# Sums of the second MLP weights: GpSimd instead of VectorE

## The chip, the cores and the metric

The kernel runs on one core of one Trainium2 chip. The metric is the device time of one execution in microseconds, the median of several runs. The core has TensorE (PE in the rows, with its weight loads as PEld), VectorE (DVE), ScalarE (ACT), GpSimd (POOL), and SyncE (SP), which in this kernel issues every DMA from one queue in the order of the program.

## What is computed

One residual block on 1024 tokens with 1024 channels: an adaLN-modulated norm, a combined input projection, two mixers (a gated linear recurrence and a short convolution), an output projection, and then the part that matters here, an MLP with 4096 hidden channels:

```
mod = silu(c) @ ada_w + ada_b                     # shift1, scale1, gate1, shift2, scale2, gate2
h   = rmsnorm(x, norm1_g) * (1 + scale1) + shift1
x   = x + gate1 * (mixers(h @ w_in) @ w_out)
h2  = rmsnorm(x, norm2_g) * (1 + scale2) + shift2
x   = x + gate2 * (square(relu(h2 @ w_mlp1)) @ w_mlp2)
out = rmsnorm(x, final_g)
```

## The kernel before

Every operand of a product is split in two float32r parts, a high one and a low one. `split` (L92 and L93) does it: ScalarE copies the source to the high part, and then VectorE writes source minus high part as the low part. Three matmuls (low weight, high weight, high weight with the low part of x; L97, L99, L101) make one product step.

Both MLP products are done by Strassen's scheme in Winograd's form. The work is cut into 16 pairs of quadruples of output tiles, `u` = 0 to 7 for the first MLP product and `u` = 8 to 15 for the second. Each pair needs seven products, P1 to P7, in the order 1, 6, 7, 4, 5, 3, 2. One product is 24 matmuls of 512 columns. The weights of a pair come as four blocks A11, A12, A21, A22, each [128, 1024] float32, and four sums of them are needed: S1 = A21 + A22, S3 = A11 - A21 and S2 = S1 - A11 in `sums`, and S4 = A12 - S2 in `sum4`. P6 takes S2, P7 takes S3, P5 takes S1 and P3 takes S4. The blocks and S1 share five buffers (G and four in F); S3 is written over A21, S2 over A11, S4 over S2. S2 can therefore only be made when A11 has been split for P1, and S4 when S2 has been split for P6.

`produce` makes the next weight operand, one for each product, into a ring of five slots. It is written when the product that used the slot five operands before has ended, so it is needed four products later.

In the second MLP product the x operands are sums of hidden tiles, which lie in DRAM (`hidd`). They are in four groups of two pairs. `load_hid` loads the next group's operands while the second pair of a group runs (u = 9, 11, 13; the first group's while u = 7 runs): for each of the seven products two halves, 14 in all, and each half is a DMA of 512 KB into one of two raw buffers, and a `split` from there. The two raw buffers are used in turn: `F[:, 24:26]` and `E[:, 2:4]`. A buffer is loaded again when VectorE has written the low part from it. These stretches are called windows below: window 1 is around u = 9, window 2 around u = 11, window 3 around u = 13; each reaches into the first products of the next pair. In a row, R<-E is the split of such a half from the E buffer. R<-F is either a half from the F buffer or a weight operand, R<-G is always a weight operand.

The result of a product stays in two PSUM banks. `acc2` (L963) on VectorE adds each bank into the residual: with P1, P6, P7 and P4 accumulating in the same two banks (as P5 and P3 do in two others), the next product may only write to a bank when `acc2` has read it. The first bank of a product is complete after half of its matmuls.

The order on each engine is not the order of the source: a list scheduler sets it with its own model of durations. Each engine then works strictly in that order.

Of the kernel before, what the change touches and what calls it, by code (L numbers as in the profile page):

```python
# [12 lines left out]
ALU = mybir.AluOpType  # L13

P = 128
# [8 lines left out]
# n-tiles of the input projection: 0-3 lx, 4-7 ly, 8-11 b, 12-15 c, 16-19 v.  # L24
# The first group is computed k-tile by k-tile while the modulation arrives.
# [3 lines left out]
# columns of the small vectors  # L29
# [6 lines left out]
def block_kernel(ctx, tc, xT, vec, adaT, winA, winB, gw, wout, w1, w2, outT):  # L36
# [8 lines left out]
    # R: operands of the products, each a pair of float32r parts; F: float32  # L45
# [7 lines left out]
    # two buffers that hold other things later  # L53
# [32 lines left out]
    def kc(k):  # L86
        """Columns of k-tile k in its half slot."""
        return slice(k % 4 * P, k % 4 * P + P)

    def split(dst, src):  # L90
        """dst: view [.., parts, ..] given as (hi, lo); the sum of the parts is src."""
        a = A(dst[0], src, AF.Copy)  # L92
        return a, V.tensor_tensor(dst[1], src, fp(dst[0]), op=ALU.subtract)  # L93

    def mm3(outs, wh, wl, start, stop, **kw):
        """outs: [(bank, x part hi, x part lo)]"""
        i = [T.matmul(b, lhsT=wl, rhs=xh, start=start, stop=False, **kw) for b, xh, xl in outs]  # L97
        for b, xh, xl in outs:
            T.matmul(b, lhsT=wh, rhs=xh, start=False, stop=False, **kw)  # L99
        for b, xh, xl in outs:  # L100
            T.matmul(b, lhsT=wh, rhs=xl, start=False, stop=stop, **kw)  # L101
        return i[0]
# [8 lines left out]
    def rsq(bank, r0, r1, n, act=nc.scalar.activation):  # L111
        # r0 = -2 n / sqrt(bank / n + EPS), one Newton step after the table
        act(r0, bank, AF.Abs_reciprocal_sqrt, bias=epsc, scale=1.0 / n)
        a = A(r1, r0, AF.Square)
        V.scalar_tensor_tensor(r1, bank, n * EPS, r1, op0=ALU.add, op1=ALU.mult)
        return a, V.scalar_tensor_tensor(r0, r1, -3.0 * n, r0, op0=ALU.add, op1=ALU.mult)
# [3 lines left out]
    def after(inst, prev):  # L120
        """inst is issued behind prev on their engine."""
        tc.add_manual_dep(ins_of(inst), ins_of(prev).name, NOSYNC, reason="order")
        return inst

# [43 lines left out]
    # softplus(a_param) = max(a, 0) + log1p(exp(-|a|))  # L168
# [19 lines left out]
    # the array clocks up while x comes in  # L188
# [9 lines left out]
    # order of adaT: (scale1, shift1) by k, gate1, (scale2, shift2) by k, gate2  # L198
# [58 lines left out]
    with tc.manual_schedule(engines={ET.DVE, ET.Activation, ET.SP}):  # L257
# [3 lines left out]
        # twice silu(c): c + c tanh(c / 2), then along the free dimension for all partitions  # L261
        cp = vt[:, V_C : V_C + KT]
        A(sc, cp, AF.Tanh, scale=0.5)
        # the table of the reciprocal root comes in before it is needed
# [13 lines left out]
        # norm1 of chunk 0: sums of squares, two tiles at a time  # L278
# [109 lines left out]
    # functions from the tables of ScalarE in one order, that keeps tables long  # L388
# [7 lines left out]
    def norm_out(n, cc, y, sqt, r1, bank, k):  # L396
        """y / rms of its group * gain, split into the slot of K-tile k."""
        A(sqt, y, AF.Square)
        dst = rs_(16 + 2 * k + cc)
        split(dst, sqt)  # L400
        T.matmul(bank, lhsT=bones, rhs=dst[0], start=True, stop=False)
        T.matmul(bank, lhsT=bones, rhs=dst[1], start=False, stop=True)  # L402
        rsq(bank, sqt, r1, 64, TA)
        V.scalar_tensor_tensor(y, y, gneg[:, n : n + 1], sqt, op0=ALU.mult, op1=ALU.mult)
        split(dst, y)
# [79 lines left out]
    # first group, chunk 0: out of PSUM, then chunk 1 with the same weights  # L485
# [103 lines left out]
    # the second gate waits for the hidden layer  # L589
# [3 lines left out]
    # ---- MLP: Strassen's products in Winograd's form, on 2 x 2 blocks of  # L593
    # (output channels) x (input channels) and (input channels) x (tokens).
    # Two quadruples of output tiles go side by side.
    # Weights: A11, A12, A21, A22; operands of the seven products:
    #   P1 A11 B11   P2 A12 B21   P3 S4 B22   P4 A22 T4   P5 S1 T1   P6 S2 T2   P7 S3 T3
    #   S1 = A21 + A22, S2 = S1 - A11, S3 = A11 - A21, S4 = A12 - S2
    #   T1 = B12 - B11, T2 = B22 - T1, T3 = B22 - B12, T4 = B21 - T2
    # first half slot and step of the operands, slots of the weights  # L600
# [4 lines left out]
    # the last pair ends on P4, P2, P5, P3, by halves of the tokens  # L605
# [12 lines left out]
    def pump():  # L618
        # keep one buffer for the sum S1 of the quadruples at hand
        while li[0] < len(loads) and comp_free:  # L620
            u, a = loads[li[0]]
            if len(comp_free) == 1 and any((v, 1) not in comp and (v, "S1 done") not in comp for v in range(u + 1) if (v, 22) in comp):
                break
            buf = comp_free.pop(0)
            kind, j = pairs[u]
            dma(buf, (w1 if kind == "w1" else w2)[j, {11: 0, 12: 1, 21: 2, 22: 3}[a]].rearrange("p (q b) -> p q b", q=2))
            comp[u, a] = buf
            li[0] += 1

    def sums(u):  # L630
        """All sums of the weights of pair u but S4."""
        if (u, 1) in comp or (u, "S1 done") in comp:
            return
        s1 = comp_free.pop(0)
        comp[u, 1] = s1
        comp[u, "S1 done"] = True
        V.tensor_tensor(s1, comp[u, 21], comp[u, 22], op=ALU.add)
        V.tensor_tensor(comp[u, 21], comp[u, 11], comp[u, 21], op=ALU.subtract)
        V.tensor_tensor(comp[u, 11], s1, comp[u, 11], op=ALU.subtract)

    def sum4(u):
        """S4, in the place of S2 or of A12, whichever is split already."""
        if (u, "S4") not in comp:
            t = comp[u, 11] if 6 in made[u] else comp[u, 12]
            V.tensor_tensor(t, comp[u, 12], comp[u, 11], op=ALU.subtract)
            comp[u, "S4"] = t
# [5 lines left out]
    def produce():  # L652
        """The next weight operand, split into the ring."""
        if wi[0] >= len(wseq):
            return
        u, p = wseq[wi[0]]
        slot = WR[wi[0] % 5]
        wslot[u, p] = slot
        wi[0] += 1
        pump()  # L660
        if p in (5, 6, 7, 3):
            sums(u)
        done = made.setdefault(u, set())
        dst = (R[:, slot : slot + 2, HI, :], R[:, slot : slot + 2, LO, :])
        if p == 3:
            sum4(u)
            split(dst, comp[u, "S4"])
        else:
            split(dst, comp[u, {1: 11, 2: 12, 4: 22, 5: 1, 6: 11, 7: 21}[p]])
        done.add(p)  # L670
        for a, users in ((11, {1, 6, 3}), (12, {2, 3}), (21, {7}), (22, {4}), (1, {5})):
            if (u, a) in comp and p in users and users <= done:
                comp_free.append(comp.pop((u, a)))
        pump()
# [4 lines left out]
    def xops(p, kp, cs=slice(0, H)):  # L679
        """Operands kp and kp + 1."""  # L680
        s0, st = XS[p]
        i = slice(s0 + kp * st, s0 + kp * st + st + 1, st)
        return R[:, i, HI, cs], R[:, i, LO, cs]

    # chunk 1 of the output projection, all but the first tile by halves of the
    # tokens; norm2 of what is done beside it
# [20 lines left out]
    def h2(cc, k, cs):  # L707
        """Tiles k and k + 1."""
# [6 lines left out]
    def t12(cs, steps):  # L715
        """h2 of chunk 1, T1, T2 and B22; steps go between."""
# [62 lines left out]
    def out_last():  # L779
        """The other half of the tokens, and the operands of the first half."""  # L780
# [165 lines left out]
    for u in range(8):  # L946
        if u == 7:
            # three pairs of tiles stay out of the last round, for x and the operands
# [23 lines left out]
    def block2(p, n0):  # L972
        """Chunk and tile that take the product p, or the sum that it ends."""
# [23 lines left out]
    # the last four products and the last norm, by halves of the tokens  # L997
# [80 lines left out]
def pack(i):  # L1078
    """Layout only: transposes, gathers of rows and columns, zero padding."""
# [28 lines left out]
    # blocks (output half, input half) of two quadruples: [pair][block][P][q][kp][P]  # L1108
    w1 = i["w_mlp1"][0].reshape(2, 4, P, 8, 2, 2, P)  # kh kp p pair q nh n
    w1 = f(w1.transpose(3, 5, 0, 2, 4, 1, 6).reshape(8, 4, P, D))  # L1110
    w2 = i["w_mlp2"][0].reshape(4, 4, 2, P, 2, 2, 2, P)  # g kp kh p half q nh n
# [22 lines left out]
```

## Time and profile before

| | us |
|---|---|
| median of 3 runs | 999.07 |
| the runs | 1000.42, 999.07, 993.2 |
| span of the profiled execution | 995.8 |
| TensorE busy in it | 968.8 |
| VectorE busy | 753.9 |
| ScalarE busy | 539.6 |
| GpSimd busy | 0.2 |

The profile's own time is given as its span alone, 995.8 us, which lies between the fastest run and the median. The page shows a busy time for each engine; it says little of a stage, since the two MLP products, the mixers and the start have different limits. The second MLP product runs from about 664 us to the end.

### The profile page before, as it was taken

How to read it: one execution, taken by the hardware profiler on the slowest of the kernel's cores; microseconds unless marked ns; L12 is line 12 of the kernel's file. 1: busy time of each engine (PE TensorE's matmuls, PEld its weight loads, DVE VectorE, ACT ScalarE, POOL GpSimd, SP SyncE). 2: the span in 40 equal slices, each digit the busy share in tenths (PEclk: the TensorE clock that was granted, in tenths of full speed). 3: DMA queues.
4: the chain of work that ended last, by engine and by line, in shares of the span. 5: the costliest groups of instructions: out<-in, count | busy, mean ns of one | idle time of the engine just before them, and what ended most of it. 6: DMA issues, size and time to landing. Idle time of an engine off the chain costs nothing.

```text
span 995.8 us, 11633 instructions
## 1 busy us (share of the span) xinstructions
PE 968.8 (97%) x4430; PEld 798.7 (80%) x4430; DVE 753.9 (76%) x1001; ACT 539.6 (54%) x719; POOL 0.2 (0%) x4
## 2 busy tenths in 40 slices
PE   8999999999999999999999999999999999999996
PEld 6878777778888988888888888887877878877886
DVE  7989788989545799776565564787797698598657
ACT  6769896874412677555455464682342253243444
POOL 0000000000000000000000000000000000000000
PEclk9999999999999999999999999999999999999999
DMA  8924015267322131773452444779554255155005
GB/s 308 345 93 146 1 44 190 67 214 262 113 106 96 49 118 58 254 271 142 155 195 101 169 169 140 282 249 321 169 180 140 97 188 180 66 188 169 1 1 168
DMA packets 53543, 154.50 MB, mean 155 GB/s; under 512 B 5104, under 2 KB 10736, under 8 KB 53488
## 3 DMA queue, kind: packets, MB, share of 16 engines
q1 hardware_dynamic: 53488, 153.77, 44.4%
q8 instruction: 34, 0.56, 0.2%
q14 instruction: 21, 0.17, 0.1%
HBM read 116.00 MB, written 37.75 MB: 154 GB/s over the span
## 4 chain that ended last, share of the span: by engine, by line
PE 69%; DMA 12%; DVE 10%; ACT 6%; issue 1%; SPq 0%; DVEq 0%; ACTq 0%
PE bank L97 23%; PE bank L99 22%; PE bank L101 22%; DMA E<-hidd 8%; DVE R L93 5%; ACT R L92 3%; DMA F<-hidd 2%; DMA F<-adaT 2%; ACT F L392 1%; DVE F L202 1%; DVE F L450 1%; DMA F<-xT 1%; DVE F L963 1%; ACT L392 1%; PE bank L402 1%
## 5 line engine op out<-in xcount | busy, mean ns | idle before, releaser
L97 PE MATMUL bank<-R 128*128 128x512 f32 (+1 forms) x1416 | 524.4, 382 | 10.7 <-DVE F L963 6.2
L99 PE MATMUL bank<-R 128*128 128x512 f32 (+1 forms) x1416 | 521.3, 379 | 0.0
L101 PE MATMUL bank<-R 128*128 128x512 f32 (+1 forms) x1416 | 516.6, 379 | 0.5 <-DVE R L93 0.5
L97 PEld LDWEIGHTS bank<-R 128*128 128x128 f32 x1416 | 266.7, 188 | 67.5 <-DVE F L963 10.8
L101 PEld LDWEIGHTS bank<-R 128*128 128x128 f32 x1416 | 266.8, 188 | 51.1 <-DVE R L93 1.0
L99 PEld LDWEIGHTS bank<-R 128*128 128x128 f32 x1416 | 266.8, 188 | 49.5 <-issue 0.7
L92 ACT ACTIVATE R<-F 128x1024 fp32r<-128x1024 f32 (+1 forms) x188 | 179.6, 965 | 178.7 <-PE bank L101 95.5
L93 DVE TENSOR_TENSOR R<-F,R 128x1024 fp32r<-128x1024 f32 (+1 forms) x188 | 205.5, 1109 | 72.4 <-ACT R L92 72.1
L963 DVE SCALAR_TENSOR_TENSOR F<-bank,md,F 128x512 f32<-128x512 f32 (+1 forms) x120 | 84.8, 712 | 36.3 <-PE bank L101 35.7
L92 ACT ACTIVATE R<-E 128x1024 fp32r<-128x1024 f32 x28 | 29.7, 1061 | 43.9 <-DMA E<-hidd 42.7
L878 ACT ACTIVATE F<-bank 128x512 f32<-128x512 f32 x44 | 26.2, 595 | 50.4 <-PE bank L101 49.1
L93 DVE TENSOR_TENSOR R<-E,R 128x1024 fp32r<-128x1024 f32 x28 | 34.3, 1224 | 12.2 <-ACT R L92 11.6
L93 DVE TENSOR_TENSOR R<-G,R 128x1024 fp32r<-128x1024 f32 x23 | 28.1, 1222 | 12.0 <-ACT R L92 12.0
L202 DVE SCALAR_TENSOR_TENSOR F<-F 128x1024 f32<-128x1024 f32 x24 | 29.2, 1221 | 4.1 <-DMA F<-adaT 4.1
L92 ACT ACTIVATE R<-G 128x1024 fp32r<-128x1024 f32 x23 | 24.2, 1054 | 11.2 <-PE bank L101 11.2
L392 ACT ACT_TABLE_LOAD x22 | 28.2, 1283 | 0.4
L567 ACT ACTIVATE E<-F 128x512 f32<-128x512 f32 (+1 forms) x21 | 11.1, 527 | 31.6 <-DVE F L565 29.6
L565 DVE SCALAR_TENSOR_TENSOR F<-bank,md,F 128x512 f32<-128x512 f32 (+1 forms) x21 | 12.7, 621 | 14.9 <-PE bank L101 14.9
L878 ACT ACTIVATE E<-bank 128x512 f32<-128x512 f32 x20 | 11.9, 594 | 21.6 <-PE bank L101 21.6
L882 ACT ACTIVATE F<-F 128x1024 f32<-128x1024 f32 x18 | 18.9, 1050 | 3.9 <-DVE F L916 2.0
L893 ACT ACTIVATE F<-bank 128x512 f32<-128x512 f32 x16 | 9.4, 596 | 19.8 <-PE bank L101 18.6
L883 ACT ACTIVATE F<-F 128x1024 f32<-128x1024 f32 x18 | 19.1, 1059 | 0.5
(196 smaller groups left out, 704.9 us busy)
## 6 DMA issues: line engine op xcount, KB each, us to landing
F<-w SPq DMA_DIRECT2D x51, 512.0 KB, 4.1
hidd<-F SPq DMA_DIRECT2D x47, 512.0 KB, 4.4
F<-adaT SPq DMA_DIRECT2D x44, 512.0 KB, 4.3
F<-hidd SPq DMA_DIRECT2D x28, 512.0 KB, 3.9
E<-hidd SPq DMA_DIRECT2D x28, 512.0 KB, 4.8
F<-xT SPq DMA_DIRECT2D x16, 512.0 KB, 5.9
F<-winB SPq DMA_DIRECT2D x13, 512.0 KB, 3.3
G<-w SPq DMA_DIRECT2D x13, 512.0 KB, 4.2
```

Source lines behind the costliest of these rows:

```text
L92: a = A(dst[0], src, AF.Copy)
L93: return a, V.tensor_tensor(dst[1], src, fp(dst[0]), op=ALU.subtract)
L97: i = [T.matmul(b, lhsT=wl, rhs=xh, start=start, stop=False, **kw) for b, xh, xl in outs]
L99: T.matmul(b, lhsT=wh, rhs=xh, start=False, stop=False, **kw)
L101: T.matmul(b, lhsT=wh, rhs=xl, start=False, stop=stop, **kw)
L202: g = V.scalar_tensor_tensor(fl(r), fl(r), 0.5, fl(cb) if cv is None else cv, op0=ALU.mult, op1=ALU.mult, accum_out=mods[:, idx : idx + 1])
L392: i = A(*args, **kw)
L565: V.scalar_tensor_tensor(x, b, gate(16, n), x, op0=ALU.mult, op1=ALU.add)
L878: A(t[:, q, :], bk2[q], AF.Copy)
L882: A(t, t, AF.Relu)
L883: A(t, t, AF.Square)
L963: V.scalar_tensor_tensor(x1(cc, n)[:, cs], b, gate(40, n), x1(cc, n)[:, cs], op0=ALU.mult, op1=ALU.add)
```

## The change

The sums S1, S2, S3 and S4 of pairs 8 to 15 are issued to GpSimd; those of pairs 0 to 7 stay on VectorE. Nothing else is edited (comments apart), but lines behind `adder` move down by five: L963 becomes L968, and the sums L637, L638, L639 and L645 become L642, L643, L644 and L650.

```
+    def adder(u):
+
+        return V if u < 8 else nc.gpsimd
+
     def sums(u):
...
-        V.tensor_tensor(s1, comp[u, 21], comp[u, 22], op=ALU.add)
-        V.tensor_tensor(comp[u, 21], comp[u, 11], comp[u, 21], op=ALU.subtract)
-        V.tensor_tensor(comp[u, 11], s1, comp[u, 11], op=ALU.subtract)
+        W = adder(u)
+        W.tensor_tensor(s1, comp[u, 21], comp[u, 22], op=ALU.add)
+        W.tensor_tensor(comp[u, 21], comp[u, 11], comp[u, 21], op=ALU.subtract)
+        W.tensor_tensor(comp[u, 11], s1, comp[u, 11], op=ALU.subtract)
 
     def sum4(u):
...
-            V.tensor_tensor(t, comp[u, 12], comp[u, 11], op=ALU.subtract)
+            adder(u).tensor_tensor(t, comp[u, 12], comp[u, 11], op=ALU.subtract)
             comp[u, "S4"] = t
```

The scheduler makes another order of it on VectorE and ScalarE; SyncE's order is the same as before. On VectorE, in the middle of window 1 (u = 9), there stood before, with three of the sums (L638 is S3, L639 is S2, L645 is S4) between splits and accumulations:

```order
L638 TENSOR_TENSOR F<-F 128x1024
L963 SCALAR_TENSOR_TENSOR F<-bank_82,md,F 128x512
L93 TENSOR_TENSOR R<-F,R 128x2x512
L639 TENSOR_TENSOR F<-F 128x1024
L93 TENSOR_TENSOR R<-E,R 128x2x512
L963 SCALAR_TENSOR_TENSOR F<-bank_83,md,F 128x512
L93 TENSOR_TENSOR R<-F,R 128x2x512
L963 SCALAR_TENSOR_TENSOR F<-bank_84,md,F 128x512
L93 TENSOR_TENSOR R<-F,R 128x2x512 x2
L93 TENSOR_TENSOR R<-E,R 128x2x512
L963 SCALAR_TENSOR_TENSOR F<-bank_83,md,F 128x512
L963 SCALAR_TENSOR_TENSOR F<-bank_84,md,F 128x512
```

In the same place there stands now:

```order
L93 TENSOR_TENSOR R<-F,R 128x2x512
L968 SCALAR_TENSOR_TENSOR F<-bank_82,md,F 128x512
L93 TENSOR_TENSOR R<-F,R 128x2x512
L968 SCALAR_TENSOR_TENSOR F<-bank_83,md,F 128x512
L93 TENSOR_TENSOR R<-E,R 128x2x512
L968 SCALAR_TENSOR_TENSOR F<-bank_84,md,F 128x512
L93 TENSOR_TENSOR R<-F,R 128x2x512 x2
L968 SCALAR_TENSOR_TENSOR F<-bank_83,md,F 128x512
L93 TENSOR_TENSOR R<-E,R 128x2x512
L968 SCALAR_TENSOR_TENSOR F<-bank_84,md,F 128x512
```

The sums are gone, and the accumulation of bank 83 (P5, first half) now stands ahead of the split from the E buffer and no longer behind it; a little later that of bank 84 has come to stand behind the next split from E.

At the end of window 1, in the first products of u = 10, VectorE's rows were before:

```order
L93 TENSOR_TENSOR R<-E,R 128x2x512
L963 SCALAR_TENSOR_TENSOR F<-bank_86,md,F 128x512
L93 TENSOR_TENSOR R<-F,R 128x2x512 x2
L963 SCALAR_TENSOR_TENSOR F<-bank_87,md,F 128x512
L963 SCALAR_TENSOR_TENSOR F<-bank_80,md,F 128x512
L93 TENSOR_TENSOR R<-E,R 128x2x512
L93 TENSOR_TENSOR R<-F,R 128x2x512
L963 SCALAR_TENSOR_TENSOR F<-bank_87,md,F 128x512
```

They are now:

```order
L93 TENSOR_TENSOR R<-E,R 128x2x512
L968 SCALAR_TENSOR_TENSOR F<-bank_86,md,F 128x512
L93 TENSOR_TENSOR R<-F,R 128x2x512 x2
L968 SCALAR_TENSOR_TENSOR F<-bank_87,md,F 128x512
L93 TENSOR_TENSOR R<-E,R 128x2x512
L968 SCALAR_TENSOR_TENSOR F<-bank_80,md,F 128x512
L93 TENSOR_TENSOR R<-F,R 128x2x512
L968 SCALAR_TENSOR_TENSOR F<-bank_87,md,F 128x512
```

The accumulation of bank 80 (P1 of u = 10, second half) has moved behind the last split from the E buffer. The same two moves are in windows 2 and 3 with other banks.

On ScalarE, in the middle of window 1, the high parts stood in this order (the first of the three in a row is the weight operand made of S2, the second that of S3, the third is a half from the F buffer):

```order
L92 ACTIVATE R<-E 128x2x512
L92 ACTIVATE R<-F 128x2x512
L92 ACTIVATE R<-E 128x2x512
L92 ACTIVATE R<-F 128x2x512 x3
L92 ACTIVATE R<-E 128x2x512
L92 ACTIVATE R<-G 128x2x512
L92 ACTIVATE R<-F 128x2x512
```

They stand now:

```order
L92 ACTIVATE R<-E 128x2x512
L92 ACTIVATE R<-F 128x2x512 x2
L92 ACTIVATE R<-E 128x2x512
L92 ACTIVATE R<-F 128x2x512 x2
L92 ACTIVATE R<-E 128x2x512
L92 ACTIVATE R<-F 128x2x512
L92 ACTIVATE R<-G 128x2x512
```

The high part made of S2 is now the second of the pair in the second row, ahead of the half from E that it stood behind.

## Rows read from the trace of the kernel before

**Rows 1.** The page's busy times of all engines over the span.

```profile
PE 968.8 (97%) x4430; PEld 798.7 (80%) x4430; DVE 753.9 (76%) x1001; ACT 539.6 (54%) x719; POOL 0.2 (0%) x4
```

**Rows 2.** Windows: stretch, length; busy us and count by engine; clock, DMA, GB/s.

```profile
664.40:705.80 41.40, 39.06 (x169) 31.20 (x168) 32.62 (x34) 14.10 (x15) 0.00 (x0) 1.00 0.80 274
705.80:746.30 40.50, 38.67 (x169) 31.38 (x168) 35.57 (x38) 19.01 (x20) 0.00 (x0) 1.00 0.54 183
746.30:785.80 39.50, 38.68 (x170) 31.39 (x168) 27.22 (x29) 10.14 (x10) 0.00 (x0) 1.00 0.36 119
705.80:943.30 237.50, 231.31 (x1009) 188.46 (x1008) 187.26 (x195) 91.59 (x92) 0.00 (x0) 1.00 0.41 140
```

**Rows 3.** Waits of TensorE, 664 to 950 us: us in total, times, longest.

```profile
PE bank L97 <- DVE F L963: 6.2, 7, 1.8
```

**Rows 4.** Timeline of TensorE: start, us, what, idle before and its releaser.

```profile
599.81 0.39 PE L97 MATMUL bank<-R 128*128 128x512 f32 x1
...
605.25 0.39 PE L97 MATMUL bank<-R 128*128 128x512 f32 x1
...
735.75 0.50 PE L97 MATMUL bank<-R 128*128 128x512 f32 x1 [1.83 <-DVE F L963]
...
758.47 0.50 PE L97 MATMUL bank<-R 128*128 128x512 f32 x1 [0.21 <-DVE F L963]
...
836.47 0.39 PE L97 MATMUL bank<-R 128*128 128x512 f32 x1
...
916.12 0.39 PE L97 MATMUL bank<-R 128*128 128x512 f32 x1
```

**Rows 5.** The chain that ended last, in window 1: start, us, what.

```profile
714.00 5.23 DMA E<-hidd
719.25 1.07 ACT R L92
...
748.40 5.88 DMA E<-hidd
754.30 1.07 ACT R L92
```

**Rows 6.** Timeline of VectorE in windows 1, 2 and 3, columns as in rows 4.

```profile
719.06 1.22 DVE L93 TENSOR_TENSOR R<-F,R 128x1024 fp32r<-128x1024 f32 x1
...
724.48 2.36 DVE L93 TENSOR_TENSOR R<-F,R 128x1024 fp32r<-128x1024 f32 x2 [0.45 <-ACT R L92]
727.63 1.23 DVE L93 TENSOR_TENSOR R<-E,R 128x1024 fp32r<-128x1024 f32 x1 [0.79 <-ACT R L92]
...
732.36 1.22 DVE L639 TENSOR_TENSOR F<-F 128x1024 f32<-128x1024 f32 x1
733.80 1.23 DVE L93 TENSOR_TENSOR R<-E,R 128x1024 fp32r<-128x1024 f32 x1 [0.23 <-ACT R L92]
734.95 0.75 DVE L963 SCALAR_TENSOR_TENSOR F<-bank,md,F 128x512 f32<-128x512 f32 x1
...
751.71 1.40 DVE L963 SCALAR_TENSOR_TENSOR F<-bank,md,F 128x512 f32<-128x512 f32 x2
755.39 1.23 DVE L93 TENSOR_TENSOR R<-E,R 128x1024 fp32r<-128x1024 f32 x1 [2.27 <-ACT R L92]
...
833.17 1.23 DVE L93 TENSOR_TENSOR R<-E,R 128x1024 fp32r<-128x1024 f32 x1 [1.68 <-ACT R L92]
...
911.92 1.23 DVE L93 TENSOR_TENSOR R<-E,R 128x1024 fp32r<-128x1024 f32 x1 [0.79 <-ACT R L92]
```

**Rows 7.** Lines of VectorE, 638 to 996 us: xcount, busy, mean ns, idle before.

```profile
L638 DVE TENSOR_TENSOR F<-F 128x1024 f32<-128x1024 f32 x6 | 7.3, 1218 | 0.0
```

**Rows 8.** Lines of ScalarE, 638 to 996 us, columns as in rows 7.

```profile
L92 ACT ACTIVATE R<-E 128x1024 fp32r<-128x1024 f32 x27 | 28.6, 1061 | 43.6 <-DMA E<-hidd 42.7 <-PE bank L99 0.9
```

**Rows 9.** Lines of GpSimd, whole span, columns as in rows 7.

```profile
L1120 POOL MEMSET const-float32-1.0<- 128x1 f32 x1 | 0.1, 98 | 0.0
```

**Rows 10.** Timeline of ScalarE in window 1, columns as in rows 4.

```profile
732.71 1.06 ACT L92 ACTIVATE R<-E 128x1024 fp32r<-128x1024 f32 x1 [2.20 <-DMA E<-hidd]
```

## Prediction

> **What bounds the kernel now.** I read the page first: TensorE is busy for 968.8 of 995.8 us, VectorE for 753.9 [rows 1]. Averages decide nothing, so next come the stretches of the second MLP product. A product of 24 matmuls takes 605.25 - 599.81 = 5.44 us where nothing disturbs it [rows 4], so a pair of seven costs 38.1 us and six pairs 228.5. Pairs 9 to 14 took 237.5, and pair 8 took 41.4 [rows 2]. So TensorE stands idle for 9.0 + 3.3 = 12.3 us in the stage that the change touches. This is also the most that any relief of VectorE can give there.
>
> Who ends these waits? VectorE's accumulations, for 6.2 us of TensorE's own idle time [rows 3]; weight loads wait beside them. VectorE was busy for 35.6 of 40.5 us in pair 9 and for 27.2 of 39.5 in pair 10 [rows 2]: nearly full in a window, not beyond its length. So I followed the chain of waits through window 1. It is one raw buffer's round, again and again: a DMA into E (5.23 us), ScalarE's high part (1.07), VectorE's low part, the next DMA, and so to the last of them (5.88, 1.07) [rows 5]. Each low part starts within 0.05 us of its high part's end: 732.71 + 1.06 = 733.77 against 733.80, and 754.30 + 1.07 = 755.37 against 755.39 [rows 5, 6, 10]. No sum of weights stands in this chain. VectorE, which works in order, **waits** for it: 2.27 us ahead of the last split [rows 6]. An accumulation that stands behind such a split waits too, and with it TensorE: the one at 734.95 came behind the split at 733.80, and TensorE went on at 735.75 after 1.83 us [rows 4, 6].
>
> **What it removes.** Four sums for each of 8 pairs, 32 at 1.22 us [rows 7], 39 us of VectorE's work. In a window this shortens nothing, because the round of the E buffer had no sum in it. Between windows VectorE has some 12 us of slack in a pair, so it gives nothing there. I cost the relief at zero. What hides it is the DMA's 4 to 6 us in each round; were the loads to come sooner, the relief would count (third rival).
>
> **What it adds on GpSimd.** The same 32 sums there. The only GpSimd row is a fill of one column in 98 ns [rows 9], so the price T must be bounded. Low end: VectorE's own 1.22 us [rows 7]. For a value I take an engine that reads its two inputs one after the other: two passes at ScalarE's one-input pace, 2 x 1.06 = 2.1 us [rows 8], an estimate. High end: twice that, 4.2. At 2.1 the four sums of a pair take 8.5 us, and an operand is due four products, 21.8 us, after its slot came free. GpSimd itself is late for nobody.
>
> The Trainium skill gives a pace for just this operation (GPSIMD Engine Reference, section 3.1): 4497 ns against VectorE's 2293 for 2048 float32, a ratio of 1.96. By it T would be an estimated 2.4 us and the forecast some 1 us higher; no row here shows it.
>
> **Sum against split.** The sums and the low parts are the same kind of work: two inputs in SBUF of 1024 columns. No row shows GpSimd and VectorE at work together. Ends: they run side by side at no cost, or one waits for the whole of the other. The nearest rows are today's: a sum ahead of a split in VectorE's queue holds it for its whole length, as 732.36 + 1.22 = 733.58 did for the split behind it, which by luck was only ready at 733.77 [rows 6, 10]. I take the second end: one at a time. The accumulations read one input from PSUM and are taken to go on.
>
> What this does in window 1, with T = 2.1: S1 can start when the split at 719.06 has freed its buffer (720.3) and, behind the E split that starts just then (high part done at 720.3 [rows 5]), runs from 721.6 to 723.7; S3 follows to 725.8. The two splits of 724.48 [rows 6] then start 1.3 us late and end at 728.1. S2 needs the second of these, starts at 728.1 and holds the E split, which was ready at 727.6, until 730.2: 2.6 us late. S4 comes where no E split is ready. A delay in the round of the E buffer is not made up, since the DMA follows at once. So 2.6 us a window; 0 if nothing collides, 2 x 2.1 = 4.2 if two sums do. Three windows: **+7.8** (0 to 12.6). Between windows the same collisions cost a split up to 2.1 us, within VectorE's slack there; zero.
>
> A rule of the skill speaks to this (SBUF — State Buffer, section Who interferes with whom): a VectorE instruction with two SBUF inputs contends with a GpSimd instruction that reads SBUF, and the later one is blocked until the other ends. By that rule the second end is the right one, by the absence of any such row here it is open; the rule changes the time by the 7.8 us already worked out.
>
> **What moves in the order.** Two accumulations change places with an E split, in each window. The first, P5's first half, goes ahead: the 1.83 us wait of window 1 goes. It is not a gain, since TensorE meets the second move: P1's second half of the next pair, which ran at 751.71 with the first half ahead of the split of 755.39 [rows 6], now comes behind that split. TensorE then waits for: split start, 1.15 to the next start (734.95 - 733.80), 0.75 accumulation, 0.06 to the matmul [rows 4, 6], then the second half of P6, 12 matmuls or 2.72 us, plus 0.27 since a matmul behind a wait shows 0.50 and not 0.23. That is 4.95 us after the split's start:
> window 1: 755.39 + 4.95 = 760.3 for the start of P7, against 758.47: +1.9;
> window 2: 833.17 + 4.95 = 838.1 against 836.47: +1.6;
> window 3: 911.92 + 4.95 = 916.9 against 916.12: +0.7 [rows 4, 6].
> These starts hold whatever went before, as the chain sets them. Sum **+4.2**. On ScalarE the high part made of S2 now stands ahead of a half from E that landed at 732.71 [rows 10]. With S2 done at 730.2 this costs nothing; it costs us for us from T = 3.5 on, about.
>
> **Sum.** 4.2 + 7.8 = 12.0 us. The profiled span of 995.8 becomes 1007.8; the profile lies 3.3 us under the median of the runs, and on the median of 999.07 it is **1011 us**.
>
> **Rivals.**
> *No collision* (the two engines share without cost): only the order counts, 999.07 + 4.2 = 1003, no difference that shows. For it: nothing in this trace forbids it. Against: both engines would have to read two float32 inputs each at once.
> *GpSimd far slower* (T = 4.2): S3 ends at 730.0, the splits of 724.48 at 732.4, S2 at 736.6; the E split of 727.6 waits until then, 9 us, and ScalarE stands behind S2's high part. 3 x 9 + 4.2 = 31, so 1030. Nothing but the absence of a row speaks for it.
> *Faster*: the loads into E come sooner than in this profile. Loads of 5.23 and 5.88 us stand in the chain [rows 5]; if each of the six rounds were 0.8 us shorter, the splits would be ready 5 us earlier, the moved accumulations would wait for nothing, and the relief of VectorE would take half of the 12.3 us: 993. The ceiling is 999 - 12 = 987. This decides only if traffic changes, and SyncE's order is the same.
> That the sums do not go to GpSimd at all is excluded by the order.
>
> **How the numbers follow.** A measurement here can tell about 1% from no change: 989 to 1009. Forecast 0.50, from 1003 to 1016 as the collisions cost 0 to 12.6; most of it (0.37) above 1009. No collision 0.26. Far slower 0.13, all above 1009. Faster 0.11, half of it below 989 at most. So slower by over 1%: 0.50; within: 0.45; faster: 0.05. The range leaves out most of the far slower case and the lower part of the faster one: 995 to 1020.
>
> **What would show it.** GpSimd rows of L642 to L650 of about 2 us; L93 rows stretched or late beside them; the E round longer in window 1 than 714 to 756.6; in each window a wait of TensorE for L968 right behind the last E split, and none at P5. Wrong if L93 keeps 1.22 us beside GpSimd's sums, if the last E split of window 1 ends earlier than 42 us after its first load, or if TensorE's idle time in pairs 9 to 14 falls below 9 us.

## The result: slower by 2.5%, 24 us where 12 were forecast

| | before | after |
|---|---|---|
| median of 4 runs, us | 997.72 | 1022.13 |
| range, us | 993.2 to 1000.42 | 1018.45 to 1022.46 |
| ratio of the times, 95% interval | | 1.0254, 1.023 to 1.0278 |
| span of the profiled execution, us | 995.8 | 1016.4 |

The fourth run of the kernel before, 996.36, is one more than the three given ahead of the prediction. The time lies 2 us above the forecast's range. The page's busy times first (as in [rows 1]):

```profile
PE 974.9 (96%) x4430; PEld 801.2 (79%) x4430; DVE 735.0 (72%) x969; ACT 540.0 (53%) x719; POOL 81.5 (8%) x36
```

VectorE lost 32 sums of 1.22 us, 39 us, but its busy time fell by 18.9 only: what it kept became longer. GpSimd's 32 sums take 81.3 us, 2.54 each. The windows of the second product (columns as in [rows 2]): pair 8, pair 9, pair 10, and pairs 9 to 14 together.

```profile
664.72:710.01 45.29, 39.88 (x170) 31.07 (x168) 28.80 (x31) 14.49 (x15) 10.46 (x4) 1.00 0.71 247
710.01:754.05 44.04, 41.29 (x169) 33.50 (x168) 34.14 (x32) 18.54 (x18) 10.48 (x4) 0.92 0.51 167
754.05:795.14 41.09, 38.68 (x169) 31.37 (x168) 23.90 (x26) 10.40 (x10) 9.64 (x4) 1.00 0.34 115
710.01:963.86 253.85, 236.55 (x1009) 191.46 (x1008) 174.57 (x170) 91.12 (x91) 60.20 (x24) 0.98 0.39 131
```

Pairs 9 to 14 went from 237.5 to 253.85 us: +16.4. Pairs 7 and 8, around the start of the stage, took 6.0 more (79.48 us before, from the first matmul of P1 of pair 7 to that of pair 9; 85.43 after). The window of pair 9 also has a granted clock of 0.92, where every window of [rows 2] had 1.00.

Who ends TensorE's waits from 640 to 970 us, and ScalarE's behind GpSimd (columns as in [rows 3]):

```profile
PE bank L97 <- DVE F L968: 20.2, 12, 2.9
...
ACT R L92 <- POOL F L644: 9.4, 3, 4.5
...
ACT R L92 <- POOL F L643: 4.2, 1, 4.2
```

The 6.2 us of [rows 3] are 20.2 now. The accumulations themselves still take 0.74 us; they come late. Why, is to be read in VectorE's and GpSimd's timelines of window 1, side by side (columns as in [rows 4]):

```profile
724.23 1.22 DVE L93 TENSOR_TENSOR R<-E,R 128x1024 fp32r<-128x1024 f32 x1
725.37 0.74 DVE L968 SCALAR_TENSOR_TENSOR F<-bank,md,F 128x512 f32<-128x512 f32 x1
728.44 2.83 DVE L93 TENSOR_TENSOR R<-F,R 128x1024 fp32r<-128x1024 f32 x1 [2.33 <-ACT R L92]
731.19 0.74 DVE L968 SCALAR_TENSOR_TENSOR F<-bank,md,F 128x512 f32<-128x512 f32 x1
...
733.65 3.02 DVE L93 TENSOR_TENSOR R<-E,R 128x1024 fp32r<-128x1024 f32 x1
```

```profile
724.41 3.31 POOL L642 TENSOR_TENSOR F<-F,G 128x1024 f32<-128x1024 f32 x1 [16.37 <-DVE R L93]
727.80 2.39 POOL L643 TENSOR_TENSOR F<-F 128x1024 f32<-128x1024 f32 x1
733.21 2.38 POOL L644 TENSOR_TENSOR F<-F 128x1024 f32<-128x1024 f32 x1 [3.02 <-DVE R L93]
```

S1 came 0.18 us after a split had begun, and took 3.31 us: the split's rest, 1.04, and then 2.3. S3 ran alone for 2.39. The split of 728.44 came into it, ended at 731.27, and had its usual 1.22 us from 730.05 on, when S3 was all but over (730.19). The split of 733.65, from the E buffer, came into S2 and ended 1.08 us after S2 did. Whoever came second waited for the whole of the first. The accumulation of 725.37, which reads a bank, ran beside S1 in its usual time.

By the Trainium skill (SBUF — State Buffer, section Who interferes with whom) a VectorE instruction with two SBUF inputs and a reading GpSimd instruction exclude each other, and the later one is blocked; the trace agrees, with 2.83 and 3.02 us for 1.22 and 3.31 for 2.39. The price that the Trainium skill states for GpSimd's addition (GPSIMD Engine Reference, section 3.1) gave an estimate of 2.4 us, against 2.39 here.

The accumulation of 731.19 stood behind the stretched split, and TensorE behind it, as its timeline shows:

```profile
728.85 0.39 PE L101 MATMUL bank<-R 128*128 128x512 f32 x1
731.98 0.80 PE L97 MATMUL bank<-R 128*128 128x512 f32 x1 [2.75 <-DVE F L968]
732.58 0.63 PE L99 MATMUL bank<-R 128*128 128x512 f32 x1
733.00 0.63 PE L101 MATMUL bank<-R 128*128 128x512 f32 x1
733.43 0.63 PE L97 MATMUL bank<-R 128*128 128x512 f32 x1
```

After this wait the matmuls start 0.43 us apart and not 0.23, until 738.1. The window there (columns as in [rows 2]) has the clock, 0.50 of full speed, that is 1.2 GHz:

```profile
732.60:738.10 5.50, 5.50 (x14) 4.27 (x13) 5.50 (x5) 1.59 (x2) 2.38 (x1) 0.50 0.27 99
```

So a wait of 2.75 us cost some 2.6 more behind it (13 matmuls, each 0.20 late). The same happened at 901.4, behind a wait of 2.9 us. Before, the longest wait for an accumulation was 1.8 us [rows 3], and no window of [rows 2] was below full clock.

Last, the end of window 1 in the chain that ended last (columns as in [rows 5]):

```profile
756.66 5.37 DMA E<-hidd
...
763.15 1.23 DVE R L93
764.38 0.67 DVE F L968
765.05 0.04 issue
765.09 0.50 PE bank L97
```

This is the move that the prediction described: TensorE goes on behind the last E split and the accumulation that was put behind it.

### The profile page after: what moved, and what is told of

Read it like the earlier page. It is cut to its first block, busy times and chain, and to the rows that moved or that the text cites. A ratio compares the mean times of both kernels' runs of the same rounds, so it can differ in the third digit from the quotient of the medians.

```text
span 1016.4 us, 11697 instructions
## 1 busy us (share of the span) xinstructions
PE 974.9 (96%) x4430; PEld 801.2 (79%) x4430; DVE 735.0 (72%) x969; ACT 540.0 (53%) x719; POOL 81.5 (8%) x36
## 4 chain that ended last, share of the span: by engine, by line
PE 71%; DMA 11%; DVE 10%; ACT 5%; issue 1%; POOL 1%; DVEq 0%; SPq 0%; ACTq 0%; POOLq 0%
PE bank L97 23%; PE bank L101 23%; PE bank L99 23%; DMA E<-hidd 7%; DVE R L93 5%; ACT R L92 2%; DMA F<-adaT 2%; DMA F<-hidd 2%; DVE F L968 1%; ACT F L392 1%; DVE F L450 1%; DVE F L202 1%; ACT L392 1%; PE bank L402 0%; DVE F L448 0%
## 5 line engine op out<-in xcount | busy, mean ns | idle before, releaser
L97 PE MATMUL bank<-R 128*128 128x512 f32 (+1 forms) x1416 | 526.7, 383 | 26.0 <-DVE F L968 20.2
L93 DVE TENSOR_TENSOR R<-F,R 128x1024 fp32r<-128x1024 f32 (+1 forms) x188 | 214.4, 1155 | 91.6 <-ACT R L92 91.3
L968 DVE SCALAR_TENSOR_TENSOR F<-bank,md,F 128x512 f32<-128x512 f32 (+1 forms) x120 | 85.2, 711 | 54.1 <-PE bank L101 53.8
L642 POOL TENSOR_TENSOR F<-F 128x1024 f32<-128x1024 f32 x3 | 7.2, 2399 | 691.5 <-DMA hidd<-F 638.1
L93 DVE TENSOR_TENSOR R<-E,R 128x1024 fp32r<-128x1024 f32 x28 | 42.9, 1531 | 18.3 <-ACT R L92 18.2
L887 ACT ACTIVATE F<-F 128x1024 f32<-128x1024 f32 x18 | 18.9, 1050 | 3.8 <-DVE F L921 2.1
```

The costliest lines, as they stand in the source:

```text
L887: A(t, t, AF.Relu)
L968: V.scalar_tensor_tensor(x1(cc, n)[:, cs], b, gate(40, n), x1(cc, n)[:, cs], op0=ALU.mult, op1=ALU.add)
```

## Experiments

Two sums over the matmul starts from 620 to 970 us make the traces comparable: **waits** (starts more than 0.55 us after the one before, less the usual 0.227; a wait counted so is 0.1 to 0.2 us longer than the idle time in its row) and **slow** (starts 0.3 to 0.55 us apart, less 0.227: half clock, and single starts at full clock, most of them right behind a wait, which make the 2.0 us of the kernel before). With them, the length of pairs 7 and 8 and of pairs 9 to 14 (from the first matmul of P1 of a pair to that of another; at full speed 24 matmuls of [rows 4] in a product make 76.2 and 228.5 us), and the median against that of the kernel before on the same chip. The medians are of several runs; the four columns on the right are of one execution each, which for the changed kernel was the fastest of four (1018.45):

| kernel | median - before, us | ratio, 95% interval | pairs 7, 8 | pairs 9-14 | waits | slow |
|---|---|---|---|---|---|---|
| before | | | 79.48 | 237.50 | 9.9 | 2.0 |
| after | 1022.13 - 997.72 = +24.4 | 1.0254 (1.023, 1.0278) | 85.43 | 253.85 | 27.1 | 6.8 |
| 1 GpSimd, order of before | 1015.24 - 998.53 = +16.7 | 1.016 (1.0112, 1.0208) | 81.58 | 255.54 | 23.1 | 8.6 |
| 2 order of after alone | 1010.12 - 998.53 = +11.6 | 1.0112 (1.0096, 1.0128) | 83.51 | 247.42 | 16.9 | 8.5 |
| 3 28 extra additions | 1017.98 - 998.53 = +19.5 | 1.02 (1.018, 1.0219) | 82.77 | 254.70 | 21.8 | 10.0 |
| 4 odd pairs on GpSimd | 1003.16 - 998.53 = +4.6 | 1.0044 (1.0027, 1.0062) | 84.36 | 238.64 | 15.5 | 2.1 |
| 5 even pairs on GpSimd | 1016.41 - 997.54 = +18.9 | 1.0182 (1.0152, 1.0211) | 80.55 | 254.32 | 21.5 | 7.9 |
| 6 28 one-input operations | 1002.95 - 997.54 = +5.4 | 1.0049 (1.0029, 1.0068) | 80.48 | 243.16 | 14.2 | 4.2 |
| 7 third buffer, VectorE | 987.53 - 997.54 = -10.0 | 0.9899 (0.9876, 0.9921) | 78.65 | 228.86 | 1.8 | 0.8 |
| 8 third buffer, GpSimd | 991.89 - 997.54 = -5.7 | 0.9941 (0.9919, 0.9963) | 81.82 | 230.86 | 6.2 | 1.2 |
| 9 third buffer, after | 1008.66 - 997.75 = +10.9 | 1.0093 (1.0063, 1.0124) | 86.48 | 241.24 | 17.1 | 5.3 |
| 10 third buffer, before | 989.07 - 997.75 = -8.7 | 0.9904 (0.9877, 0.9932) | 79.68 | 229.29 | 2.3 | 1.6 |

Waits and slow starts account for the changed kernel: 17.2 + 4.8 = 22.0 us of the 22.3 that pairs 7 to 14 became longer.

### 1. GpSimd's sums in the order of the kernel before

The changed kernel, with a line of order-only dependences through the instructions of VectorE, ScalarE and TensorE, so that each engine issues them as before:

```
+    rows = {"DVE": [(638, 639), (625, 626), (651, 652),
...
+    for e, spans in rows.items():
+        line = [issued[e][i] for a, b in spans for i in range(a, b)]
+        for x, y in zip(line, line[1:]):
+            after(y, x)
```

> The late sums are on GpSimd as in the changed kernel, but VectorE, ScalarE and TensorE issue everything else in the order of the kernel before, row for row. What is left is what GpSimd's sums do by themselves: they hold VectorE's subtractions up and take longer than VectorE's. Theory A (the prediction's step d, enlarged: the moved accumulations let TensorE wait for a split that is itself held up, and one of the three moves was missed): the time falls by a half of the 24 us or more, to 1006 to 1012 us, and the waits of TensorE at the first product of a pair and the clock's fall to 1.2 GHz in the first and the third window are gone. Rival B (latency: what TensorE waits for is a sum of 2.4 to 3.4 us ahead of ScalarE's high parts, whatever the order): 1018 to 1023 us. Rival C (the order was everything): 996 to 1001 us.

Measured +16.7, between theory A and rival B, since the interval (+11 to +21 us) takes in both. The wait before P7 of pair 8 went, as A said. But the waits before P6 of pairs 12 and 14 (2.2 and 2.8 us) did not, nor did the halved clock: it comes in window 1 and in window 2 and the tail of 3, for instance behind the wait before P3 of pair 9 (TensorE's timeline, columns as in [rows 4], and the window, columns as in [rows 2]; with the order written out every instruction has the helper's line, L79):

```profile
736.93 0.80 PE L79 MATMUL bank<-R 128*128 128x512 f32 x1 [3.16 <-DVE F L79]
```

```profile
737.50:743.10 5.60, 5.60 (x15) 4.32 (x14) 5.60 (x5) 1.64 (x2) 2.36 (x1) 0.50 0.35 114
```

The moved order is not needed to make the sums dear; by themselves they cost some twice the 7.8 us of the prediction.

### 2. The order alone

The kernel before, sums on VectorE, with the same kind of line for the order of the changed kernel.

```
+    rows = {"DVE": [(638, 639), (625, 626), (647, 648),
...
```

> The sums stay on VectorE, but all other instructions of VectorE, ScalarE and TensorE stand in the changed kernel's order, row for row. This is the order's cost without GpSimd. The prediction put it at 4.2 us (1.9, 1.6 and 0.7 in the three windows). Theory A: each of the some ten moved accumulations makes TensorE wait for one split of 1.2 us, of which a part lies beside other waits: 3 to 8 us over the kernel before, 1001 to 1006 us. Rival C (the order was everything): 1015 to 1022 us. Rival D (the order costs only where a split is stretched by GpSimd): within 2 us of the kernel before.

Measured +11.6: above A's range, below C's. Waits grew by 7.0 us, which is A's figure, and slow starts by 6.5, which nobody had counted. The waits: 2.03 us before P7 of pair 8, where before had none, and 2.2 and 1.6 before P6 of pairs 10 and 12 (0.77 and 0.46 before). The wait before P3 of pair 9, which the prediction let go with the first move, is still there (2.10 us, 1.99 before). Alone, the two parts make 16.7 + 11.6 = 28.3; together 24.4. That fits waits which both lengthen (in pairs 9 to 14 the sums cost 18.0, the order 9.9 and both together 16.4 us), but the first experiment's interval is as wide as the difference, so it is not shown.

### 3. Additions that nobody waits for

```
+            if p in (1, 6, 4, 5) and u < 15:
+                cc, n = block2(p, 4 * half)
+                two = F[:, cc * 8 + n : cc * 8 + n + 3 : 2, :]
+                extra.append(nc.gpsimd.tensor_tensor(E[:, 0:2, :H], two, two, op=ALU.add))
...
```

> The kernel before with its sums on VectorE, and four additions more for each pair from the ninth to the fifteenth on GpSimd, 28 in all, of the sums' shape, 128 x 1024 float32, that read two accumulated tiles and write a buffer that nobody reads; one behind each of four products of a pair. Orders are those of before but for one ScalarE split near the end. No one waits for these additions, so what they cost is that GpSimd and VectorE can't do such operations at one time. Theory A: VectorE's subtractions and sums that meet one take up to 3.1 us and not 1.2, the rest does not change; 4 to 12 us over the kernel before. Rival B (the cost of the change is the length of GpSimd's sums on the path, not the holding up): within 2 us of the kernel before, though single subtractions are stretched.

Measured +19.5, far from B and over A's range. This is the plainest proof that the holding up alone is dear: nothing reads these additions, no row moved on VectorE or TensorE, and the kernel lost most of what the change lost. (One ScalarE operation, at 947.59 in pair 14, waits 1.8 us for an addition to have read its tile; TensorE has no wait over 0.9 us behind it in that pair.) The additions fall at other places than the sums, and read one pair of tiles twice, for which one alone takes 1.89 us and not 2.39; so this run shows the mechanism and not the size of the change's own loss. In the groups by line (columns as in [rows 7]) the splits carry it and the accumulations don't:

```profile
L991 POOL TENSOR_TENSOR E<-F 128x1024 f32<-128x1024 f32 x28 | 67.9, 2425 | 885.9 <-DMA hidd<-E 676.2 <-DVE F L963 209.7
```

```profile
L93 DVE TENSOR_TENSOR R<-F,R 128x1024 fp32r<-128x1024 f32 (+1 forms) x188 | 225.6, 1214 | 66.8 <-ACT R L92 66.4
L963 DVE SCALAR_TENSOR_TENSOR F<-bank,md,F 128x512 f32<-128x512 f32 (+1 forms) x120 | 84.1, 709 | 35.9 <-PE bank L101 35.7
L93 DVE TENSOR_TENSOR R<-E,R 128x1024 fp32r<-128x1024 f32 x28 | 40.0, 1429 | 7.7 <-ACT R L92 7.5
```

Of the splits from 640 to 970 us, 18 took over 1.5 us, up to 2.92, and lost 26.5 us in all (15 and 20.9 us in the first experiment; none before).

### 4 and 5. Half of the pairs each

```
-        return V if u < 8 else nc.gpsimd
+        return nc.gpsimd if u in (9, 11, 13, 15) else V
```

> GpSimd makes the late sums of the second pair of each quadruple alone (pairs 9, 11, 13 and 15 counted from 0), which fall beside the pairs ahead of the windows, when no hidden tiles are loaded and split; VectorE makes the others, which fall into the windows and to the start of the stage. By the prediction (collisions count in the windows alone, nothing between them): within 3 us of the kernel before. By the pairs of the changed kernel's trace, added up (3.9 for pair 8, 1.6, 3.6 and 1.7 for pairs 10, 12 and 14): 1006 to 1010 us.

```
+        return nc.gpsimd if u in (8, 10, 12, 14) else V
```

> The other half of the fourth experiment: GpSimd makes the late sums of the first pair of each quadruple alone (pairs 8, 10, 12 and 14), those of 8 at the start of the stage and the others inside the three windows; VectorE makes those of the odd pairs. Theory A as the prediction had it (the windows pay): nearly all of the changed kernel's loss is here, 1014 to 1022 us, and TensorE waits before the last two products of each window's pair and the first of the next. If loss follows the number of sums, wherever they stand: 1004 to 1008 us, as with the odd pairs.

Measured +4.6 and +18.9, together 23.5, nearly the whole loss; the fourth lies between its two forecasts, the fifth in theory A's range. The sums of odd pairs, made when no hidden tiles come in, cost pairs 9 to 14 only 238.64 - 237.50 = 1.1 us, and pair 8 4.1. With those of even pairs, made inside the windows, pairs 9 to 14 lost 16.8 us. These two runs split the loss by place and not by cause: the order was not held. Apart from the sums, VectorE's and ScalarE's rows of the fourth stand in the order of before but for two splits, at 690 and 710 us, and those of the fifth in the changed kernel's order but for two rows. What the moved order does to the fifth is settled by the first experiment: in the order of before, all sums cost pairs 9 to 14 18.0 us, of which the odd ones, by the fourth, make 1.1. So the sums inside the windows cost some 17 us there in either order. Adding up the pairs of the changed kernel misled me: what pairs 10, 12 and 14 lost there they lost to the tail of the window ahead of them. The prediction's zero between windows holds.

### 6. One input instead of two

```
-                extra.append(nc.gpsimd.tensor_tensor(E[:, 0:2, :H], two, two, op=ALU.add))
+                extra.append(nc.gpsimd.tensor_scalar(E[:, 0:2, :H], two, 2.0, None, op0=ALU.mult))
```

> The third experiment with one thing changed: the 28 extra operations of GpSimd multiply one input by 2 (128 x 1024 float32 in, 128 x 1024 out) where there two inputs were added. Nothing waits for them. If any GpSimd work that touches the same memory holds VectorE's subtractions up, they stay stretched to 2 to 3 us beside one and the time is again 10 us or more over the kernel before. If it is an operation with two inputs that VectorE and GpSimd can't do at one time, VectorE's subtractions stay at 1.22 us and the time is within 3 us of the kernel before, 996 to 1003 us.

Measured +5.4 by the medians. The 1002.95 lies just inside the second case's 996 to 1003, but neither case holds: the splits did not stay at 1.22 us, and 5.4 is more than 3. The splits are held, but for less: 20 took over 1.5 us, none over 2.06, and 15.2 us were lost where two inputs cost 26.5. So one input on GpSimd is not free beside VectorE either, but it cost less, though the operation is longer itself (2.77 us alone).

### 7 and 8. A third raw buffer

```
-            t = XR[xr[0] % 2]
+            bufs = XR if g == 0 else XR + [E[:, 0:2, :H]]
+            t = bufs[xr[0] % len(bufs)]
```

with the rows of VectorE, ScalarE and TensorE held in the order of before; once with all sums on VectorE, once with the late ones on GpSimd.

> The kernel before (all sums on VectorE, the order of VectorE, ScalarE and TensorE kept row for row) with a third raw buffer for the hidden tiles in the three windows, which lies free there. The prediction said that the round of the two raw buffers (transfer, high part, low part, next transfer) bounds the windows, and that relief of VectorE is worth nothing there for this reason. If so, TensorE's waits before the last product of a window's pair (1.99, 0.70 and 1.36 us in the profile of before) and at the first products of the pair behind it go, some 3 to 7 us: 991 to 995 us. If the waits have another cause (order of VectorE's rows, ScalarE), within 1.5 us of the kernel before.

> The first experiment (late sums on GpSimd, everything else in the order of the kernel before) with the third raw buffer. If GpSimd's sums cost time because the splits that they hold up stand in the round of two buffers, the round now has slack and most of the 17 us are gone: 998 to 1004 us. If they cost it because TensorE waits for operands and accumulations behind a held up subtraction whatever the buffers, 1011 to 1016 us.

Measured 987.53 and 991.89, both better than their ranges: the third buffer gave 10.0 us, where 3 to 7 were expected. The windows of the seventh experiment (columns as in [rows 2]) for pairs 9, 10, and 9 to 14:

```profile
702.80:741.20 38.40, 38.37 (x170) 31.45 (x169) 35.32 (x38) 19.68 (x20) 0.00 (x0) 1.00 0.58 187
741.20:779.30 38.10, 38.10 (x169) 31.45 (x168) 27.19 (x29) 9.57 (x9) 0.00 (x0) 1.00 0.39 129
702.80:931.60 228.80, 228.77 (x1009) 189.06 (x1008) 186.03 (x195) 91.32 (x92) 0.00 (x0) 1.00 0.44 143
```

and of the eighth:

```profile
707.65:746.74 39.09, 38.42 (x169) 31.38 (x168) 36.02 (x34) 19.95 (x20) 12.21 (x4) 1.00 0.57 182
...
707.65:938.51 230.86, 229.70 (x1010) 188.69 (x1008) 175.16 (x171) 92.18 (x92) 63.74 (x24) 1.00 0.43 141
```

TensorE is never idle in the windows of the seventh, with VectorE as busy as before (35.32 us of a pair of 38.40, against 35.57 of 40.50 in [rows 2]). So it was not VectorE's load that bound them, but the round of two buffers. The eighth holds as many splits up as the first experiment did, 15, by 20.6 us in all, and yet loses 4.4 us against the seventh, not 16.7. The hold-ups cost what they cost because they fell into that round.

### 9 and 10. The third buffer in the scheduler's own order

The same edit, on the changed kernel and on the kernel before, without the order written out.

> The changed kernel with the third raw buffer and the order that the scheduler then makes of itself. If the round of two buffers turns both the held up splits and the moved accumulations into TensorE's waits, both are nearly free now: 990 to 997 us, where the changed kernel took 1022. If the moved accumulations cost something of their own (the wait before the third product of pair 8, 3.09 us, has no transfer in it), a part stays: 997 to 1002 us.

> The kernel before with the third raw buffer alone and the scheduler's own order, two lines of change; the seventh experiment kept the rows of before by hand. TensorE waited 1.8 us in all between its products there, so nothing is left for an order to win: 985 to 990 us. If the scheduler again moves accumulations behind splits, as it did in the changed kernel, up to 8 us more.

Measured 1008.66 and 989.07. The tenth is as good as the seventh to 1.5 us, with one line of the kernel before turned into two. The ninth missed its first case and lies above its second: it differs from the eighth in the order of rows alone, and that is worth 16.8 us. (SyncE's order differs too, in 18 of 319 rows, but the tenth has the same one and stands 1.5 us from the seventh.) In its window 1, ScalarE's, GpSimd's and TensorE's timelines (columns as in [rows 4]) show the kind of row that does it:

```profile
736.33 1.06 ACT L92 ACTIVATE R<-F 128x1024 fp32r<-128x1024 f32 x1 [2.16 <-POOL F L644]
```

```profile
733.91 2.39 POOL L644 TENSOR_TENSOR F<-F 128x1024 f32<-128x1024 f32 x1 [2.36 <-DVE R L93]
```

```profile
741.03 0.50 PE L97 MATMUL bank<-R 128*128 128x512 f32 x1 [2.57 <-DVE F L969]
```

ScalarE waits for S2, two splits of VectorE (737.97, 2.34 us) wait for ScalarE, an accumulation stands behind them at 740.24, and TensorE goes on at 741.03 after 2.57 us.

## Why the prediction was half right

The mechanism held; three terms of the sum failed. The collisions were put at 7.8 us and cost 16.7, the moved order was put at 4.2 and cost 11.6 alone, and the start of the stage was put at nothing and cost 6.0. The last two overlap: with the order alone pairs 7 and 8 lost 4.0.

**The bound (right).** That the round of the raw buffers bounds the windows is shown by the seventh and eighth experiments. That relief of VectorE is worth nothing there was argued from the chain, and no run relieved VectorE without giving GpSimd the work. The prediction's ceiling for the faster side was 12.3 us, TensorE's whole idle time in the stage; the third buffer gave 10.0 of it.

**The price of a sum (right in kind).** Taken 2.1 us, measured 2.39 alone. The prediction's remark that 2.4 us would make the forecast some 1 us higher was wrong by its own steps: in a window S1, S3 and S2 stand behind one another ahead of the E split, so 0.3 us more for a sum is 0.9 us more in each window and 2.7 in three.

**One at a time (right), 7.8 us (mis-sized; 16.7 by the first experiment, with +11 to +21).** The step counted one late E split in each window, 2.6 us. In the first experiment's trace the splits that were held number 15 and lose 20.9 us. Ten of them, with 16.8 us, lie in the windows: two in the first and four in each of the others. And the step had no term for what follows a long wait: slow starts grew by 6.6 us in that experiment. Some 10 us are left without them.

**Zero between windows and at the start (half wrong).** Between windows it held (fourth experiment, 1.1 us). At the start of the stage it failed by 6.0 us: 2.1 in pair 7 and 3.9 in pair 8. In pair 7 the first group's hidden tiles are loaded, as in a window, while GpSimd makes the sums of pair 8; the prediction counted three windows and not this one. VectorE's and TensorE's timelines there show a split held beside S3 and, later, a wait that the kernel before did not have; between them lies the round of the E buffer (its split at 644.45, then a transfer of 5.45 us):

```profile
641.37 3.16 DVE L93 TENSOR_TENSOR R<-F,R 128x1024 fp32r<-128x1024 f32 x1 [2.90 <-ACT R L92]
```

```profile
653.70 0.50 PE L97 MATMUL bank<-R 128*128 128x512 f32 x1 [1.76 <-ACT F L883]
```

In pair 8 the sum's own length stands on the path, which the prediction had put aside, since "an operand is due four products" later. The changed kernel's timelines of VectorE, ScalarE and GpSimd at P7 of pair 8 (columns as in [rows 4]):

```profile
689.99 1.23 DVE L93 TENSOR_TENSOR R<-F,R 128x1024 fp32r<-128x1024 f32 x1 [3.37 <-ACT R L92]
691.13 2.06 DVE L968 SCALAR_TENSOR_TENSOR F<-bank,md,F 128x512 f32<-128x512 f32 x3
```

```profile
688.90 1.06 ACT L92 ACTIVATE R<-F 128x1024 fp32r<-128x1024 f32 x1 [4.16 <-POOL F L643]
```

```profile
683.14 2.40 POOL L642 TENSOR_TENSOR G<-F 128x1024 f32<-128x1024 f32 x1 [27.41 <-DVE R L93]
685.61 3.25 POOL L643 TENSOR_TENSOR F<-F 128x1024 f32<-128x1024 f32 x1
```

S1 and S3 end at 688.86, the high part of S3 at 689.96, its low part at 691.22, and three accumulations that were put behind it follow, with TensorE idle for 2.92 us until 691.93. S3, of pair 9, was wanted only when P7 of that pair began, at 720.89; the accumulations behind it were wanted at once. The second experiment, with VectorE's short sums in the same order, still waits 2.03 us here, and the first, with GpSimd's sums in the old order, does not. So most of this wait is a move of the order that the prediction did not price, lengthened by GpSimd's sums.

**The order, 4.2 us (mis-sized; 11.6 alone by the second experiment).** The rule for the three moves was good: the last E split of window 1 started at 763.15, plus 4.95 gives 768.10 for P7, and P7 began at 767.94; in windows 2 and 3 the rule gives 852.47 and 936.80, and P7 began at 852.32 and 936.66. But there were more moves: the accumulations ahead of P7 of pair 8, and in the changed kernel one of P7's own in window 1, at 731.19, behind which TensorE waited 2.75 us and the clock was halved. ScalarE's moved high part of S2 was put at nothing, as S2 would be done at 730.2; S2 ended at 735.59, and ScalarE stood 9.4 us in three waits for it (the row of L644 above). How much of that reached TensorE is not separated. And in the second experiment half of the cost was again the clock: 6.5 us of slow starts beside 7.0 of waits.

**The rivals.** No collision is out by the third experiment; GpSimd far slower is out by 2.39 us, though its 1030 was nearer to the result (8 us off) than the forecast of 1011 (11 us off), by luck. The forecast's upper end of 1016 came from two terms that both lacked the clock, and a third that was set to zero.

**What stays open.** How much of the 16.7 us is the length of the sums and how much the holding up is not separated; the third experiment shows that holding up is enough. Why some long waits of TensorE were followed by the halved clock and others were not is not known from these runs. Why the list scheduler chose the poorer order when the sums moved was not tried.

## What to carry to other kernels

Before work is moved off a busy engine, see whether that engine stands in the chain that bounds the stage; here it waited inside a round of two buffers, and a third buffer (one line turned into two) took 8.7 us off where the move added 24. In these traces additions on GpSimd and two-input work of VectorE on SBUF exclude each other (splits of 1.22 us became up to 3.42), so such a move gives the work back as waits, at twice the length (2.39 us for 1.22), and to whichever operation comes second. And a move that gives a scheduler other durations changes the order of rows that were not edited: compare the orders in full, and price each row that now stands behind a slower one.

## What the hardware showed that I had not expected

A wait of TensorE can cost more than its length: after 2.75 us of it the granted clock was 0.50 in the window of the next 5.5 us (1.2 and not 2.4 GHz). This came with some waits of over 2 us and not with others: 2 of the 6 in the changed kernel, 4 of the 6 in the first experiment.

GpSimd's one-input operation excluded VectorE's splits for a part of its length only. Alone it took 2.77 us; a split that came 0.2 us after its start took 1.93, so that it had its usual 1.22 from 0.9 us after the start on, while the changed kernel's addition with two inputs held one for nearly the whole 2.39. The sixth experiment's rows of GpSimd and VectorE (columns as in [rows 4]):

```profile
690.13 2.77 POOL L991 TENSOR_SCALAR E<-F 128x1024 f32<-128x1024 f32 x1 [9.18 <-DVE F L963]
699.92 6.02 POOL L991 TENSOR_SCALAR E<-F 128x1024 f32<-128x1024 f32 x2 [7.02 <-DVE F L963]
```

```profile
700.11 1.93 DVE L93 TENSOR_TENSOR R<-F,R 128x1024 fp32r<-128x1024 f32 x1 [0.34 <-ACT R L92]
```
